# The opening of a fused hybrid-mixer step: modulation weights read in 512-column blocks, x and z weights behind them, z weights in pairs

## The chip, the cores and the metric

The kernel runs on one core of a Trainium2 chip. The metric is the device time of one execution in microseconds (us). Three runs of the kernel before took 2195.02, 2198.10 and 2202.01 us, the median 2198.1. Five engines work beside each other, each taking its own instructions in the order written: TensorE (PE), VectorE (DVE), ScalarE (ACT), GpSimd (POOL) and SyncE (SP), which issues most DMAs.

## What is computed

One layer for 2048 sample tokens and 128 prompt tokens, model width 1024. The part that matters here:

```python
def ada_mod(cvec, w, b):
    m = jnp.einsum('...d,de->...e', jax.nn.silu(cvec), w) + b
    return jnp.split(m, 3, axis=-1)                    # shift, scale, gate
...
xn = rmsnorm(h, ln_g[l]) * (1.0 + scale) + shift
...
proj = jnp.einsum('btd,de->bte', xn, w_in)             # one projection for everything
qkv, beta, dec, z_a, u_b, v_b, z_b, x_c, z_c, gates = jnp.split(proj, points, axis=-1)
qkv = short_conv(qkv, conv_w)                          # three taps along the tokens, then SiLU
...
o = rmsnorm(o, o_norm_g) * jax.nn.silu(z_a)            # z_a: 512 columns of w_in
```

Behind it stand a gated delta scan with decays made from `dec`, a spatial gating branch, a Fourier branch, the branch merge and the output projection. Shift and scale come from 1024 x 2048 numbers of `w_ada` and two condition vectors; every product of tokens and weights needs them first.

## The kernel before, in words

Tokens are processed in five tiles (`TBS`): four of 512 and one of 128. A float32 matrix enters TensorE as two float16 parts, so that one product is three matmuls: hi by hi, hi by lo, lo by hi. The token side is `xh` and `xl`, the weight side `w.hi` and `w.lo`.

**Stage one, the modulation** (the loop over `blk`). `w_ada` is read in eight blocks of 256 columns, each in two DMAs of 512 KB into one of eight `ast` buffers. TensorE multiplies the tiles by the condition (`scT`); for the blocks in `AD` the second tile is summed on VectorE instead (`ada_sum`) and brought in by two matmuls with `sel`. The first token tile is read in the middle, after block 4. `ms` (scale) and `sh` (shift) follow.

**Stage two, tokens and z** (the loop over `TBS`). For each token tile ScalarE squares (L451), POOL takes the power (L171), VectorE scales (L455), TensorE transposes in eight steps k (L459), VectorE applies scale and shift (`xm`, L461, three buffers), ScalarE rounds to `xh` (L462) and POOL subtracts to `xl` (L463). Then four z blocks of 128 columns are multiplied (L161) and their SiLU is stored to DRAM (`sz`).

**Stage three, q, k and v** (the loop over `ct`, twelve blocks of 128 columns). A block is 24 matmuls (8 steps by three) for each of five token tiles, the evacuation to `raw` (L635), three VectorE instructions for the convolution (L638, L639, L640, to `cy`), four Sigmoid pieces (L643, on ScalarE) and a POOL product. Beside it runs `decays()`, in pieces that `pace` doles out: matmuls with `bdp`, then 17 tiles of two 128x1024 VectorE instructions (L610, L611), one Exp (L598) and a DMA. Its Exp and the Sigmoid need different ScalarE tables, so tables are reloaded between them.

**Weights.** Every weight block is loaded to `wst` (two buffers, freed when converted), squared on ScalarE (L209), given a scale by a few tiny VectorE instructions and one TensorE matmul with `ones`, then converted: `hi` on ScalarE (L222), `lo` on VectorE (L223). `converting` is a generator; `weight_step`, `getw`, `fetch` and `ahead` decide when its steps are issued in the program.

**Order.** What one engine does first is not what the text says first: a scheduler puts the instructions of each engine in order when the program is built, from priorities (program order, with `tc.high_priority` ahead) and its own estimate of time. On the chip each engine then keeps to that order. `tc.issue_after(x)` holds a DMA behind another instruction.

Of the kernel before, what the change touches and what calls it, by code (L numbers as in the profile page):

```python
# [11 lines left out]
F16 = mybir.dt.float16  # L12
# [8 lines left out]
P = 128  # L21
D = 1024
KT = 8
# [88 lines left out]
def hybrid_flow_kernel(ctx: ExitStack, tc: tile.TileContext, x_prompt, x_sample, state_delta, c, c_ctx, ln_g, w_ada,  # L112
# [47 lines left out]
    def mm(out, l, r, start=True, stop=True):  # L160
        PE.matmul(out, l, r, start=start, stop=stop)  # L161

    def mm3(out, l, r):
# [2 lines left out]
        mm(out, l[0], r[1], False, False)  # L166
        mm(out, l[1], r[0], False, True)

    def rsqrt(out, ss, mul, w):
        V.tensor_scalar(out, ss, mul, EPS, ALU.mult, ALU.add)  # L170
        G.tensor_tensor(out, out, mhalf.to_broadcast([P, w]), ALU.pow)  # L171
# [18 lines left out]
    def load_w(src, nkt, cols=P, hi=None, lo=None, tag="w", bufs=5):  # L190
        return convert(read_w(src, nkt, cols, tag), nkt, cols, hi, lo, tag, bufs)

    def read_w(src, nkt, cols=P, tag="w"):
        st = sb(wp, [P, nkt, cols], "wst" if cols == P else tag + "st", bufs=2 if cols == P else 1)
        SY.dma_start(st, src.rearrange("(k p) c -> p k c", p=P))
        return st

    def converting(w, st, nkt, cols=P, hi=None, lo=None, tag="w", bufs=5):

        wpool = bwp[0] if tag == "b" else wp  # L200
        if tag == "z":
            hi, lo = [sb(p0p, [P, nkt, cols], n_, F16, bufs=4) for n_ in ("zhi", "zlo")]
# [19 lines left out]
        A.activation(w.hi, st, AF.Copy, scale=s)  # L222
        V.scalar_tensor_tensor(w.lo, st, s, w.hi, ALU.mult, ALU.subtract)  # L223
# [27 lines left out]
    def xrows(t0, n):  # L251
        return xs_[t0:t0 + n, :] if t0 < NS else xp_[t0 - NS:t0 - NS + n, :]

    wlist = []
    for c0 in [C_ZA + g * P for g in range(4)]:
        wlist.append((w_in_[:, c0:c0 + P], KT, "z", 4))
# [134 lines left out]
    def load_x(t0, tn):  # L391
        xt = sb(p0p, [P, tn // P, D], "xt")
        SY.dma_start(xt, xrows(t0, tn).rearrange("(j p) d -> p j d", p=P))
        xts[t0] = xt

    for blk in range(8):
        if blk == XB:
            load_x(*TBS[0])
            columns()
        ps = bank(ps_d, [2, 256])  # L400
        for k0 in range(0, KT, 4):
            st = sb(p0p, [P, 4, 256], "ast", bufs=8)
            last_ada = SY.dma_start(st, w_ada_[k0 * P:(k0 + 4) * P, blk * 256:(blk + 1) * 256].rearrange("(k p) c -> p k c", p=P))
            if k0 and blk in AD:
                acc = sb(p0p, [P, 2, 256], "aacc")
                ada_sum(acc, st, range(k0, k0 + 4))
                for g in range(2):
                    mm(ps, sel[:, g, :], acc[:, g, :], False, g == 1)
                continue
            for k in range(4):  # L410
                mm(ps, scT[:, k0 + k, :], st[:, k, :], k0 + k == 0, k0 + k == KT - 1)
        adr = sb(p0p, [2, 256], "adr")
        V.tensor_copy(adr, ps)
        for k in range(2):
            PE.transpose(pa[:, blk * 2 + k, :], adr[:, k * P:(k + 1) * P], ident[:2, :2])
    ms = sb(cp, [P, KT, 2], "ms")
    sh = sb(cp, [P, KT, 2], "sh")
    with tc.high_priority():
# [12 lines left out]


    szD = dram("sz", [H, P, NTOK])
    with tc.issue_after(last_ada.ins):
        read_next()
        read_next()
        load_x(*TBS[1])
        zaw = getw(4)
        bdp = sb(wp, [P, KT, 32], "bdp", F16, bufs=1)
        bdw = load_w(w_in_[:, C_BD:C_BD + 16], KT, 16, hi=bdp[:, :, 0:16], lo=bdp[:, :, 16:32], tag="d")  # L440
    szlate = []
    for ti, (t0, tn) in enumerate(TBS):
        if t0 not in xts:
            load_x(t0, tn)
        g = 0 if t0 < NS else 1
        nt = tn // P
        xt = xts[t0]
        jk = sb(p0p, [P, D], "jk", F16, bufs=1)
        xss = sb(p0p, [P, nt], "xss")
        for j in range(nt):  # L450
            A.activation(jk, xt[:, j, :], AF.Square, accum_out=xss[:, j:j + 1])  # L451
        rs = sb(p0p, [P, nt], "rs")
        rsqrt(rs, xss, 1.0 / D, nt)
        for j in range(nt):
            V.tensor_scalar(xt[:, j, :], xt[:, j, :], rs[:, j:j + 1], None, ALU.mult)  # L455
        for k in range(KT):
            ps = bank(ps_d, [P, tn])
            for j in range(nt):
                PE.transpose(ps[:, j * P:(j + 1) * P], xt[:, j, k * P:(k + 1) * P], ident)  # L459
            t = sb(p0p, [P, tn], "xm", bufs=3)  # L460
            V.tensor_scalar(t, ps, ms[:, k, g:g + 1], sh[:, k, g:g + 1], ALU.mult, ALU.add)  # L461
            A.copy(xh[:, k, t0:t0 + tn], t)  # L462
            G.tensor_tensor(xl[:, k, t0:t0 + tn], t, xh[:, k, t0:t0 + tn], ALU.subtract)  # L463
        for g in range(4):
            ps = bank(ps_d if tn == P and g % 2 else ps_mm, [P, tn])
            gemm_T(ps, zaw[g], 0, xh[:, :, t0:t0 + tn], xl[:, :, t0:t0 + tn])
            sg = sb(ep, [P, tn], "sg", bufs=4)
            A.activation(sg, ps, AF.Sigmoid, scale=zaw[g].inv)
            V.scalar_tensor_tensor(sg, ps, zaw[g].inv, sg, ALU.mult, ALU.mult)
            if szlate:  # L470
                SY.dma_start(*szlate.pop())
            szlate.append((szD[g, :, t0:t0 + tn], sg))
    SY.dma_start(*szlate.pop())
    p0.close()
    ahead(2)
# [173 lines left out]
    SY.dma_start(wsn, w_spatial[0].rearrange("g p q -> p g q"))  # L649
    pace.drain()  # L650
    a1.close()

# [909 lines left out]
```

## Time and profile before

| | |
|---|---|
| runs | 2195.02, 2198.10, 2202.01 us; median 2198.1 us |
| profiled execution | 2200.34 us, of which 2198.2 us are the span of the instructions |
| TensorE | 97% busy |
| VectorE, ScalarE, POOL | 60%, 46%, 32% busy |
| DMA | 365.09 MB, mean 166 GB/s |

Times inside the program count from the start of the span. A row of a timeline gives start, duration, engine, source line, operation, tiles written <- tiles read, shape, count and, in brackets, how long the engine had been idle and what ended that. A row of "windows" gives a stretch, its length, the busy time and count of PE, PEld (weight loads), DVE, ACT and POOL, the granted TensorE clock, the busy share of the DMA engines and GB/s. A row of the waits gives who waited for whom: total, times, longest.

### The profile page before, as it was taken

The page shows a single profiled execution, that of the slowest core. Times are in us where ns is not written, and L with a number is a line of the kernel's source. Part 1 is how long each engine was busy: PE and PEld are TensorE (multiplying, and loading weights), DVE is VectorE, ACT ScalarE, POOL GpSimd, SP SyncE. Part 2 cuts the span into 40 slices and gives each one's busy share as a digit, 9 for nine tenths or more (in the row PEclk, how much of TensorE's full clock was granted, in tenths as well). Part 3 has the DMA queues.
Part 4 walks back from the last instruction along what each step waited for, and adds up shares of the span by engine and source line. Part 5 has one row for each costly group of instructions (what it writes and reads, how often), then busy time and mean ns, then how long its engine had stood idle before and what let it go on. Part 6 is the DMA issues. An engine that isn't in the chain of part 4 may idle for free. (4 is left out here: it accounts for less than half of the span.)

```text
span 2198.2 us, 42667 instructions
## 1 busy us (share of the span) xinstructions
PE 2125.9 (97%) x16234; PEld 1213.1 (55%) x16234; DVE 1311.2 (60%) x3140; ACT 1014.4 (46%) x2345; POOL 707.5 (32%) x862
## 2 busy tenths in 40 slices
PE   7999999999999999899899999999999999999998
PEld 3565444455555587777555555555654444444443
DVE  5746745469979698466665555765674544223454
ACT  3644644345466474355544445655553422222332
POOL 1421433223333322432322223344532221222543
PEclk9999999999999999999999999999999999999999
DMA  8324733167777662444655556776664544324542
GB/s 280 141 87 149 260 117 110 61 203 231 241 229 239 198 192 83 126 130 137 203 172 162 164 164 185 240 212 209 200 198 151 168 125 133 118 78 123 174 148 103
DMA packets 304568, 365.09 MB, mean 166 GB/s; under 512 B 39426, under 2 KB 215787, under 8 KB 302315
## 3 DMA queue, kind: packets, MB, share of 16 engines
q1 hardware_dynamic: 289226, 302.19, 45.6%
q0 software_dynamic: 12688, 51.27, 6.4%
q10 hardware_dynamic: 2448, 8.91, 1.0%
q8 instruction: 127, 2.08, 0.4%
q14 instruction: 79, 0.64, 0.1%
HBM read 234.67 MB, written 127.62 MB: 165 GB/s over the span
## 5 line engine op out<-in xcount | busy, mean ns | idle before, releaser
L161 PE MATMUL b<-xh,whi 128*128 128x512 f16 (+1 forms) x1920 | 652.8, 349 | 0.4 <-DVE mrow L1391 0.4
L161 PE MATMUL b<-xl,whi 128*128 128x512 f16 (+1 forms) x1920 | 652.9, 348 | 0.0
L161 PE MATMUL b<-xh,wlo 128*128 128x512 f16 (+1 forms) x1920 | 651.9, 348 | 0.5 <-DVE wlo L223 0.5
L161 PEld LDWEIGHTS <-whi 128*128 128x128 f16 x3904 | 358.8, 98 | 330.0 <-issue 9.4
L161 PEld LDWEIGHTS <-wlo 128*128 128x128 f16 x1952 | 191.7, 98 | 180.8 <-issue 5.0
L161 PE MATMUL b<-big,bhi 128*128 128x512 f16 (+1 forms) x960 | 250.6, 347 | 2.4 <-ACT big L1355 1.9
L1395 POOL TENSOR_TENSOR mrow<-mrow,sg 128x512 f32<-128x512 f32 (+1 forms) x80 | 91.8, 1148 | 293.9 <-DVE sg L1394 225.7
L161 PE MATMUL b<-big,blo 128*128 128x512 f16 (+1 forms) x480 | 162.9, 347 | 0.0
L1385 ACT ACTIVATE sg<-b,winv 128x512 f32<-128x512 f32 (+1 forms) x120 | 74.1, 618 | 174.5 <-PE b L161 173.7
L644 POOL TENSOR_TENSOR cy<-cy,raw 128x545 f32<-128x545 f32 (+1 forms) x48 | 74.9, 1586 | 184.2 <-ACT raw L643 184.2
L161 PEld LDWEIGHTS <-xh 128*128 128x128 f16 x1496 | 117.0, 98 | 28.1
L1394 DVE SCALAR_TENSOR_TENSOR sg<-b,binv,sg 128x512 f32<-128x512 f32 (+1 forms) x80 | 53.4, 667 | 126.1 <-PE b L161 119.3
L161 PEld LDWEIGHTS <-bhi 128*128 128x128 f16 x960 | 86.5, 98 | 73.6 <-issue 2.1
L175 DVE CAST wscb<-wss 128x1 bf16<-128x1 f32 x93 | 14.3, 154 | 148.5 <-ACT wlo L209 67.3
L864 POOL COPY T<-ES 32x256 f16<-32x256 f16 x68 | 30.5, 449 | 202.3 <-DMA ES<-ei 167.1
L161 PE MATMUL b<-whi,xh 128*128 128x128 f16 x544 | 92.9, 219 | 0.0
L161 PE MATMUL b<-wlo,xh 128*128 128x128 f16 x544 | 92.9, 219 | 0.0
L161 PE MATMUL b<-whi,xl 128*128 128x128 f16 x544 | 92.9, 219 | 0.0
L161 PE MATMUL b<-wohi,mh 128*128 128x512 f16 x240 | 90.9, 379 | 1.4 <-ACT mh L1462 1.4
L161 PE MATMUL b<-wohi,ml 128*128 128x512 f16 x240 | 90.8, 379 | 0.3 <-DVE mscb L175 0.3
L161 PE MATMUL b<-wolo,mh 128*128 128x512 f16 x240 | 90.9, 379 | 0.0
L209 ACT ACTIVATE wlo<-wst 128x1024 f16<-128x1024 f32 x52 | 55.0, 1057 | 77.5 <-DMA wst<-in_w_in_dram 74.1
(456 smaller groups left out, 4285.4 us busy)
## 6 DMA issues: line engine op xcount, KB each, us to landing
wst<-in_w_in_dram SPq DMA_DIRECT2D x60, 512.0 KB, 4.9
qkv<-cy POOLq DMA_DIRECT2D x12, 1089.0 KB, 5.4
st<-br SPq DMA_DIRECT2D x48, 256.0 KB, 4.6
mrow<-mrg SPq DMA_DIRECT2D x18, 512.0 KB, 3.6
mrow<-mrg SPq DMA_DIRECT2D x16, 576.0 KB
mrg<-mrow POOLq DMA_DIRECT2D x16, 576.0 KB, 3.6
dc<-dec SPq DMA_DIRECT2D x17, 512.0 KB, 4.7
kq<-qkv SPq DMA_DIRECT2D x34, 256.0 KB, 4.6
```

The lines of the kernel that those rows point to most:

```text
L161: PE.matmul(out, l, r, start=start, stop=stop)
L175: V.tensor_copy(sb16, ss)
L209: A.activation(w.lo, st, AF.Square, accum_out=ss)
L644: G.tensor_tensor(y[:, c0:c1], y[:, c0:c1], raw[:, 1 + c0:1 + c1], ALU.mult)
L864: G.tensor_copy(T16[rows(a0, b), :, :, b], ES[0:32, :, 2 * a0 + b, :, wT])
L1385: A.activation(sg, ps, AF.Sigmoid, scale=gw.inv)
L1394: V.scalar_tensor_tensor(sg, ps, binv[:, 1:2], sg, ALU.mult, ALU.mult)
L1395: G.tensor_tensor(mr, mr, sg, ALU.add)
```

## The change

- The modulation is read in four blocks of 512 columns, each in four DMAs of two row groups (still 512 KB, rows of 2 KB instead of 1 KB). Of blocks 0 and 2 three of four tiles are summed on VectorE (before: one of two tiles of every other 256-column block).
- The first token tile is read after the modulation, in four pieces. Behind it come the z weights, in two pairs of 256 columns read into `ast` buffers (`read_z`), the second token tile, the weights for the decays, and only then (`issue_after(first[0])`) the first q block's weights.
- A pair of z blocks has one common scale and is converted in two halves (`convert_z`). For the first tile both blocks of a pair go through the contraction together.
- The squares of the next token tile, of the z weights and of the first q weights are pinned behind the ten ScalarE instructions before them in the program (`pinned`); the next tile is normalised after the first z block of the present one.

The core of the diff:

```diff
-XB = 4
-AD = (0, 2, 4, 6)
+AD = (0, 2)
...
+    def pinned(made, n=10):
+        ins = made.ins
+        before = (i for i in reversed(nc.cur_bb.bb.instructions) if i is not ins and i.engine == ins.engine)
+        for _, i in zip(range(n), before):
+            tc.add_manual_dep(ins, i.name, mybir.DependencyInfo(mybir.DependencyClass.NoSync, mybir.DependencyReason.DATA),
+                              reason="pinned")
+        return made
...
-        SY.dma_start(st, src.rearrange("(k p) c -> p k c", p=P))
+        with tc.issue_after(first[0]) if len(wread) < 8 and first else ExitStack():
+            SY.dma_start(st, src.rearrange("(k p) c -> p k c", p=P))
...
-        A.activation(w.lo, st, AF.Square, accum_out=ss)
+        sq = A.activation(w.lo, st, AF.Square, accum_out=ss)
+        if wnext[0] < 6:
+            pinned(sq)
...
-    for blk in range(8):
-        if blk == XB:
-            load_x(*TBS[0])
+    for blk in range(4):
+        if blk == 2:
             columns()
-        ps = bank(ps_d, [2, 256])
-        for k0 in range(0, KT, 4):
-            st = sb(p0p, [P, 4, 256], "ast", bufs=8)
+        ps = bank(ps_d, [2, 512])
+        acc = sb(p0p, [P, 2, 512], "aacc", bufs=1) if blk in AD else None
+        for k0 in range(0, KT, 2):
+            st = sb(p0p, [P, 2, 512], "ast", bufs=8)
...
-            if k0 and blk in AD:
+            if k0 and acc is not None:
+                ada_sum(acc, st, range(k0, k0 + 2), k0 == 2)
...
+    def convert_z(sts):
+        hi, lo = [sb(p0p, [P, KT, 256], n_, F16) for n_ in ("zhi", "zlo")]
+        ss = sb(p0p, [P, 3], "zss")
+        halves = [slice(4 * h, 4 * h + 4) for h in range(2)]
+        for h, kk in enumerate(halves):
+            pinned(A.activation(lo[:, kk, :], sts[h], AF.Square, accum_out=ss[:, h:h + 1]))
+        V.tensor_add(ss[:, 2:3], ss[:, 0:1], ss[:, 1:2])
+        s, inv = scales(ss[:, 2:3], wp, "wsc")
...
     with tc.issue_after(last_ada.ins):
-        read_next()
-        read_next()
+        xt = sb(p0p, [P, 4, D], "xt")
+        for j in range(4):
+            SY.dma_start(xt[:, j, :], xrows(j * P, P))
+        xts[0] = xt
+        zst = [read_z(0), read_z(1)]
         load_x(*TBS[1])
-        zaw = getw(4)
...
+    fetch(4)
...
+        convert_z(zst[1])
+        for g0 in (0, 2):
+            pss = [bank(ps_mm, [P, tn]) for _ in range(2)]
+            for k in range(KT):
+                x_ = [t_[:, k, t0:t0 + tn] for t_ in (xh, xl)]
+                for i in range(2):
+                    mm(pss[i], zaw[g0 + i].hi[:, k, :], x_[0], k == 0, False)
+                    mm(pss[i], zaw[g0 + i].lo[:, k, :], x_[0], False, False)
+                for i in range(2):
+                    mm(pss[i], zaw[g0 + i].hi[:, k, :], x_[1], False, k == KT - 1)
+            if g0 == 0:
+                xt = next_x(ti)
```

The rebuilt order differs from the start of the program up to the middle of stage three; from the fourth q block's first tile to the end the instructions of TensorE stand as before. Lines move by up to 83: L161 becomes L160, L222 and L223 become L231 and L232, L610 and L611 become L692 and L693, L635 becomes L717, L638 to L640 become L720 to L722, L643 becomes L725.

**First place: the weights of the third q block (`ct` 2) on ScalarE and VectorE.** Before, ScalarE converts them (`whi_1984`, and the fourth block's `whi_2168`) in stage two, during the third and fourth token tile:

```order
L468 ACTIVATE sg_979<-b_954,winv_367 128x512
L462 CAST xh_93<-xm_1032 128x512
L462 CAST xh_93<-xm_1041 128x512
L462 CAST xh_93<-xm_1050 128x512
L222 ACTIVATE whi_1984<-wst_1848,wsc_2080 128x1024
L222 ACTIVATE whi_2168<-wst_2034,wsc_2263 128x1024
L468 ACTIVATE sg_1008<-b_983,winv_386 128x512
```

Now ScalarE converts the same two blocks (`whi_1911`, `whi_2095`) in stage three, behind the Sigmoid pieces of the second q block (`cy_2144`) and an Exp of the decays (`XB`):

```order
L725 ACT_TABLE_LOAD
L725 ACTIVATE raw_1931<-cy_2144 128x545 x3
L725 ACTIVATE raw_1931<-cy_2144 128x543
L680 ACT_TABLE_LOAD
L680 ACTIVATE XB_1874<-XB_1874 128x1024
L231 ACTIVATE whi_1911<-wst_1775,wsc_2007 128x1024
L680 ACTIVATE XB_1874<-XB_1874 128x1024
L231 ACTIVATE whi_2095<-wst_1961,wsc_2190 128x1024
```

The two conversions have moved by more than sixty ScalarE rows, from before the first q block to after the second one's Sigmoid.

VectorE before, from the second block's last convolution instruction (`cy_2217`) on, has no weight block until the third block's own convolution:

```order
L640 SCALAR_TENSOR_TENSOR cy_2217<-raw_2004,pc_108,cy_2217 128x2178
L611 TENSOR_TENSOR XB_1947<-XB_1947,cst_87 128x1024 x2
L610 TENSOR_TENSOR dc_2038<-dc_2038,tok_1768 128x1024
L610 TENSOR_TENSOR dc_2045<-dc_2045,tok_1768 128x1024
L611 TENSOR_TENSOR dc_2038<-dc_2038,cst_87 128x1024
L611 TENSOR_TENSOR dc_2045<-dc_2045,cst_87 128x1024
L610 TENSOR_TENSOR E_2087<-E_2087,tok_1768 128x1024
```

VectorE now, from the second row behind that convolution instruction (the row between is one more L693 on `XB_1874`) to the third block's `lo` part (`wlo_1912`):

```order
L194 TENSOR_SCALAR wsc_2007<-wsc_2007 128x1
L195 TENSOR_SCALAR wsc_2007<-wsc_2007 128x1
L693 TENSOR_TENSOR XB_1874<-XB_1874,cst_87 128x1024
L194 TENSOR_SCALAR wsc_2190<-wsc_2190 128x1
L195 TENSOR_SCALAR wsc_2190<-wsc_2190 128x1
L692 TENSOR_TENSOR dc_1965<-dc_1965,tok_1695 128x1024
L692 TENSOR_TENSOR dc_1972<-dc_1972,tok_1695 128x1024
L229 TENSOR_TENSOR winv_2012<-wsc_2007,xsc_246 128x1
L229 TENSOR_TENSOR winv_2195<-wsc_2190,xsc_246 128x1
L693 TENSOR_TENSOR dc_1965<-dc_1965,cst_87 128x1024
L692 TENSOR_TENSOR E_2014<-E_2014,tok_1695 128x1024
L232 SCALAR_TENSOR_TENSOR wlo_1912<-wst_1775,wsc_2007,whi_1911 128x1024
```

The `lo` part now stands behind six instructions of the decays that follow the second block's convolution, the last of them on a fresh `E` tile. On TensorE the third block still follows the second at once; of its matmuls the first two (hi by `xh`, hi by `xl`) of each of its five tiles and of the fourth block's first tile now stand ahead of the first one that reads `wlo_1912`.

**Second place: the weights of the first q block (`ct` 0) on ScalarE.** Before, they were converted in stage two, and at the start of stage three ScalarE has the Exp on `al` (a small parameter that is loaded there) and evacuations:

```order
L468 ACTIVATE sg_1384<-b_1359,winv_386 128x128
L540 ACT_TABLE_LOAD
L540 ACTIVATE al_1772<-al_1772 128x8
L635 ACTIVATE raw_1452<-b_1456,winv_1448 128x512
L523 COPY sq_1486<-b_1487 128x144
L523 COPY sq_1486<-b_1634 128x128
```

Now the conversion stands behind that Exp:

```order
L216 ACTIVATE wlo_1361,wss_1362<-wst_1358 128x1024
L622 ACT_TABLE_LOAD
L622 ACTIVATE al_1699<-al_1699 128x8
L605 COPY sq_1413<-b_1414 128x144
L231 ACTIVATE whi_1360<-wst_1358,wsc_1368 128x1024
L717 ACTIVATE raw_1377<-b_1381,winv_1373 128x512
```

The square and the `hi` part of the first q block have moved from stage two to behind the last z block. On TensorE most of the decays' `bdp` matmuls now stand ahead of the first block's matmuls instead of behind its first tile.

More of the change, by code (lines that the diff above doesn't have):

```diff
@@ L252, in xrows @@
         return xs_[t0:t0 + n, :] if t0 < NS else xp_[t0 - NS:t0 - NS + n, :]
-    wlist = []
-    for c0 in [C_ZA + g * P for g in range(4)]:
-        wlist.append((w_in_[:, c0:c0 + P], KT, "z", 4))
+    wlist, first = [], []
+    wlist.extend([None] * 4)
     for c0 in ([C_QKV + i * P for i in range(12)] + [C_V + g * P for g in range(4)]
@@ L433, in hybrid_flow_kernel, with read_z @@
     szD = dram("sz", [H, P, NTOK])
-    with tc.issue_after(last_ada.ins):
-        read_next()
-        read_next()
+    def read_z(pair):
+        sts = []
+        for h in range(2):
+            st = sb(p0p, [P, 4, 256], "ast", bufs=8)
+            first[:] = [SY.dma_start(st, w_in_[h * 512:(h + 1) * 512, C_ZA + pair * 256:C_ZA + (pair + 1) * 256].rearrange("(k p) c -> p k c", p=P)).ins]
+            sts.append(st)
+        return sts
+    def convert_z(sts):
[6 more added lines that the diff above has]
+        s, inv = scales(ss[:, 2:3], wp, "wsc")
+        zinv = sb(wp, [P, 1], "winv", bufs=10)
+        V.tensor_mul(zinv, inv, isx)
+        for h, kk in enumerate(halves):
+            A.activation(hi[:, kk, :], sts[h], AF.Copy, scale=s)
+            V.scalar_tensor_tensor(lo[:, kk, :], sts[h], s, hi[:, kk, :], ALU.mult, ALU.subtract)
+        for i in range(2):
+            w = _W()
+            w.hi, w.lo, w.inv = hi[:, :, i * P:(i + 1) * P], lo[:, :, i * P:(i + 1) * P], zinv
+            zaw.append(w)
@@ L437, in hybrid_flow_kernel @@
+    zaw = []
+    with tc.issue_after(last_ada.ins):
+        xt = sb(p0p, [P, 4, D], "xt")
[3 more added lines that the diff above has]
+        zst = [read_z(0), read_z(1)]
         load_x(*TBS[1])
-        zaw = getw(4)
         bdp = sb(wp, [P, KT, 32], "bdp", F16, bufs=1)
-        bdw = load_w(w_in_[:, C_BD:C_BD + 16], KT, 16, hi=bdp[:, :, 0:16], lo=bdp[:, :, 16:32], tag="d")
-    szlate = []
[L442 to L446, printed above, removed]
+        bdst = read_w(w_in_[:, C_BD:C_BD + 16], KT, 16, "d")
@@ L447, in hybrid_flow_kernel, with normed @@
+    wdone.extend([None] * 4)
+    wread.extend([None] * 4)
+    wnext[0] = 4
+    fetch(4)
+    szlate = []
+    def normed(t0, tn, step):
         xt = xts[t0]
         jk = sb(p0p, [P, D], "jk", F16, bufs=1)
[L449 to L472, printed above, removed]
+        for j0 in range(0, tn // P, step):
+            js = range(j0, min(j0 + step, tn // P))
+            xss = sb(p0p, [P, len(js)], "xss")
+            for j in js:
+                sq = A.activation(jk, xt[:, j, :], AF.Square, accum_out=xss[:, j - j0:j - j0 + 1])
+                if t0:
+                    pinned(sq)
+            rs = sb(p0p, [P, len(js)], "rs")
+            rsqrt(rs, xss, 1.0 / D, len(js))
+            for j in js:
+                V.tensor_scalar(xt[:, j, :], xt[:, j, :], rs[:, j - j0:j - j0 + 1], None, ALU.mult)
@@ new lines, in normed, with z_out, next_x @@
+        return xt
+    def z_out(g, t0, tn, ps):
+        sg = sb(ep, [P, tn], "sg", bufs=4)
+        A.activation(sg, ps, AF.Sigmoid, scale=zaw[g].inv)
+        V.scalar_tensor_tensor(sg, ps, zaw[g].inv, sg, ALU.mult, ALU.mult)
+        if szlate:
+            SY.dma_start(*szlate.pop())
+        szlate.append((szD[g, :, t0:t0 + tn], sg))
+    def next_x(ti):
+        if ti + 1 == len(TBS):
+            return None
+        if TBS[ti + 1][0] not in xts:
+            load_x(*TBS[ti + 1])
+        return normed(*TBS[ti + 1], 4)
@@ new lines, in hybrid_flow_kernel @@
+    xt = normed(*TBS[0], 2)
+    with tc.high_priority():
+        convert_z(zst[0])
+    for ti, (t0, tn) in enumerate(TBS):
+        m = 0 if t0 < NS else 1
+        nt = tn // P
+        with tc.high_priority() if ti == 0 else ExitStack():
+            for k in range(KT):
+                ps = bank(ps_d, [P, tn])
+                for j in range(nt):
+                    PE.transpose(ps[:, j * P:(j + 1) * P], xt[:, j, k * P:(k + 1) * P], ident)
+                t = sb(p0p, [P, tn], "xm", bufs=3)
+                V.tensor_scalar(t, ps, ms[:, k, m:m + 1], sh[:, k, m:m + 1], ALU.mult, ALU.add)
+                A.copy(xh[:, k, t0:t0 + tn], t)
+                G.tensor_tensor(xl[:, k, t0:t0 + tn], t, xh[:, k, t0:t0 + tn], ALU.subtract)
+        if ti:
+            for g in range(4):
+                ps = bank(ps_d if tn == P and g % 2 else ps_mm, [P, tn])
+                gemm_T(ps, zaw[g], 0, xh[:, :, t0:t0 + tn], xl[:, :, t0:t0 + tn])
+                z_out(g, t0, tn, ps)
+                if g == 0:
+                    xt = next_x(ti)
+            if ti == 1:
+                bdw = convert(bdst, KT, 16, hi=bdp[:, :, 0:16], lo=bdp[:, :, 16:32], tag="d")
+            continue
+        convert_z(zst[1])
+        for g0 in (0, 2):
+            pss = [bank(ps_mm, [P, tn]) for _ in range(2)]
+            for k in range(KT):
+                x_ = [t_[:, k, t0:t0 + tn] for t_ in (xh, xl)]
+                for i in range(2):
+                    mm(pss[i], zaw[g0 + i].hi[:, k, :], x_[0], k == 0, False)
+                    mm(pss[i], zaw[g0 + i].lo[:, k, :], x_[0], False, False)
+                for i in range(2):
+                    mm(pss[i], zaw[g0 + i].hi[:, k, :], x_[1], False, k == KT - 1)
+            if g0 == 0:
+                xt = next_x(ti)
+            for i in range(2):
+                z_out(g0 + i, t0, tn, pss[i])
@@ L648, in hybrid_flow_kernel @@
     wsn = sb(ep, [P, WB], "st", bufs=3).rearrange("p (g q) -> p g q", g=4)
-    SY.dma_start(wsn, w_spatial[0].rearrange("g p q -> p g q"))
+    with tc.issue_after(first[0]):
+        SY.dma_start(wsn, w_spatial[0].rearrange("g p q -> p g q"))
     pace.drain()
```

19 lines of the change are left out of this document (8 added, 11 removed).

## The prediction, made blind

> **What bounds the kernel now.** I read the page's engine rows first, then TensorE's waits, then windows over the part that the change touches.
>
> ```profile
> span 2198.2 us, 42667 instructions
> PE 2125.9 (97%) x16234; PEld 1213.1 (55%) x16234; DVE 1311.2 (60%) x3140; ACT 1014.4 (46%) x2345; POOL 707.5 (32%) x862
> 0.00:64.00 64.00, 47.30 (x218) 21.07 (x219) 36.30 (x94) 23.19 (x43) 14.84 (x19) 0.97 0.84 275
> 64.00:260.00 196.00, 196.00 (x1347) 105.08 (x1346) 122.49 (x179) 104.88 (x161) 65.25 (x60) 1.00 0.46 151
> PE b L161 <- DVE wlo L223: 0.5, 1, 0.5
> 200.00:220.00 20.00, 20.00 (x112) 9.82 (x111) 19.53 (x14) 13.45 (x17) 8.06 (x4) 1.00 0.77 249
> ```
>
> TensorE is the bound, so a microsecond in which it waits is a microsecond of the program. The first 64 us are the exception: DMA share 0.84, and most of the busy matmuls are the small modulation ones. From 64 to 260 us TensorE has no gap, and in the waits of 64 to 300 us there is one of 0.5 us (fifth row). But beside it VectorE is nearly full at 200 to 220 us (19.53 of 20). The kernel gets away with that because no weight that TensorE needs next stands behind VectorE's backlog. That is what the change alters, so my sum has a small term at the start and a large one there.
>
> **Part one: the start.** It has to bring 0.4 MB of constants, 8.4 MB of modulation and 2.1 MB of the first token tile, before and now. The rates:
>
> ```profile
> 0.00:8.00 8.00, 1.16 (x4) 0.51 (x5) 0.17 (x1) 1.47 (x2) 0.61 (x9) 1.00 0.66 213
> 8.00:16.00 8.00, 8.00 (x27) 2.47 (x26) 3.60 (x10) 0.00 (x0) 0.00 (x0) 1.00 1.10 351
> 16.00:22.00 6.00, 6.00 (x31) 2.45 (x30) 3.11 (x8) 0.00 (x0) 0.00 (x0) 1.00 1.04 396
> 58.00:62.00 4.00, 3.46 (x19) 1.64 (x16) 4.00 (x3) 1.44 (x6) 4.00 (x3) 1.00 1.02 419
> 23.26 1.06 ACT L451 ACTIVATE jk<-xt 128x1024 f16<-128x1024 f32 x1 [18.54 <-DMA xt<-in_x_sample_dram]
> 28.24 1.18 POOL L171 TENSOR_TENSOR rs<-rs,mhalf 128x4 f32<-128x4 f32 x1 [27.03 <-DVE rs L170]
> 29.45 2.74 DVE L455 TENSOR_SCALAR xt<-xt,rs 128x1024 f32<-128x1024 f32 x4
> 43.65 0.17 DVE L420 TENSOR_TENSOR sh<-b,pc 128x16 f32<-128x16 f32 x1 [0.84 <-PE b L415]
> 46.22 0.80 DVE L461 TENSOR_SCALAR xm<-b,ms,sh 128x512 f32<-128x512 f32 x1
> 48.65 6.62 POOL L463 TENSOR_TENSOR xl<-xm,xh 128x512 f16<-128x512 f32 x4 [19.23 <-ACT xh L462]
> 63.14 0.38 PE L161 MATMUL b<-xl,zhi 128*128 128x512 f16 x1
> ```
>
> Rows of 1 KB move at 351 GB/s (8 to 16 us, modulation alone), rows of 4 KB at 419 (58 to 62 us, a token tile): 46.7 and 156.4 ns a row on 16 engines. On the line between them 2 KB take 83.3 ns, 393 GB/s. By 8 us 1.7 MB had moved; the rest of the modulation then ends at 8 + 7.1/0.393 = 26.1 us, the token tile at 31.1, the first z pair (1 KB rows) at 34.1. What has moved is used some 1.8 us later: 6.7 MB stand ahead of the token tile's first use now, moved by 21.5 us and used at 23.26. So the tile's last quarter is usable at 32.9. Then, in VectorE's new order: a square 1.2, the power (1.18) with a 0.64 us copy of modulation rows ahead of it 2.0, two scalings 1.4 (2.74 for four), and the 2.6 from `sh` to `xm` (43.65 to 46.22): first `xm` at 40.1 instead of 46.2.
>
> Of these 6 us little reaches TensorE. ScalarE now squares the z weights only behind the bound on `ms` and `sh` (2 x 1.2 us), so the first `xl` starts at about 42.0. `xm` has three buffers, each freed by its `xl`; VectorE's order has the seventh `xm` ahead of the first z `lo` part, so that part waits for four `xl` (1.2 to 1.65 us each by the POOL row), one `xm` and 1.27 us: 49 to 51. From there 46 matmuls of the first pair, 48 of the second and 32 transposes are left, at 0.216 and 0.109 us each (the step from 206.04 to 206.26, and some 1.1 us for the ten transposes at 99.17, both below). Before, TensorE had done the first pair and nine of the transposes at 63.1, so in the same terms the work was left at 63.1 - 9.9 - 1.0 = 52.2 us. TensorE is also cold then:
>
> ```profile
> 46.00:48.00 2.00, 0.92 (x5) 0.80 (x6) 2.00 (x9) 2.00 (x4) 0.00 (x0) 0.75 0.00 0
> 48.00:50.00 2.00, 2.00 (x10) 1.74 (x10) 2.00 (x3) 2.00 (x4) 1.35 (x1) 0.50 0.00 0
> 50.00:52.00 2.00, 1.68 (x7) 0.50 (x5) 2.00 (x3) 2.00 (x5) 2.00 (x2) 0.90 0.43 100
> ```
>
> After a thin stretch its granted clock falls to 0.50 and needs some 3.4 us of work to recover, which costs 1.7 us where matmuls are waiting, as they will be now. Term: 50 + 1.7 - 52.2 = **-0.5** (from -6, the lead of `xm` kept whole, to +2).
>
> A rule speaks against the longer rows. The Trainium skill, "DMA: Bandwidth & Descriptors", section "Where 436 GB/s comes from", has about 358 GB/s per core bind for reads from HBM. By it the modulation would end about 2 us later than I have it; the 419 GB/s above, a read from HBM, disagrees.
>
> **Part two: the tile borders.** Before, the second and fourth token tiles were transposed ahead of the last z block of the tile before; now every tile is transposed after it. The one large border that already had that order:
>
> ```profile
> 99.17 1.25 PE L459 MATMUL b<-cst,xt 128*128 128x128 f32 x10
> 101.11 0.59 PE L161 MATMUL b<-xh,zhi 128*128 128x512 f16 x2
> 102.34 0.38 PE L161 MATMUL b<-xl,zhi 128*128 128x512 f16 x1
> ```
>
> Here 3.2 us pass for 2.7 us of work. With the first step's transposes, an `xm` (0.8) and an `xh` (0.6) all ahead of the first matmul I put 0.8 at three borders and 0.3 at the small tile, less the 0.5 there now: **+2.2** (0 to 4).
>
> **Part three: the first q block's weights.** Their `hi` part now stands behind the Exp on `al`:
>
> ```profile
> 159.03 1.28 ACT L540 ACT_TABLE_LOAD   x1 [4.16 <-DMA al<-in_a_log_dram]
> 154.24 0.22 PE L161 MATMUL b<-xh,zlo 128*128 128x128 f16 x1
> L161 PE MATMUL b<-bdp,xl x68: 169/169/169, 162.8 to 166.2; 128*128 128x16 f16 x68
> L161 PE MATMUL b<-bdp,xh x67: 176/176/176, 162.9 to 166.2; 128*128 128x32 f16 x67
> ```
>
> The load of `al` is issued behind the last `sz` store, so it comes no earlier against the end of stage two: `al` at 159.0, table 1.28, Exp 0.2, copy 0.3, `hi` 1.14: 161.9. TensorE has 192 `bdp` matmuls of 0.025 us to do from 154.3, that is to 159.1, and then waits: **+2.8** (0 to 5).
>
> **Part four: the third q block's weights.** This is the prediction's weight. Rows of before, around the end of the second q block:
>
> ```profile
> 205.99 0.22 PE L161 MATMUL b<-xh,wlo 128*128 128x128 f16 x1
> 206.04 0.38 PE L161 MATMUL b<-xh,whi 128*128 128x512 f16 x1
> 206.26 0.38 PE L161 MATMUL b<-xl,whi 128*128 128x512 f16 x1
> 191.53 2.36 DVE L610 TENSOR_TENSOR dc<-dc,tok 128x1024 f32<-128x1024 f32 x2 [6.82 <-DMA dc<-gamR]
> 212.97 2.24 DVE L638 TENSOR_SCALAR cy<-raw,pc 128x2178 f32<-128x2178 f32 x1
> 215.19 2.10 DVE L611 TENSOR_TENSOR dc<-dc,cst 128x1024 f32<-128x1024 f32 x1
> 226.01 2.48 DVE L640 SCALAR_TENSOR_TENSOR cy<-raw,pc,cy 128x2178 f32<-128x2178 f32 x1
> 237.04 1.45 DVE L610 TENSOR_TENSOR E<-E,tok 128x1024 f32<-128x1024 f32 x1 [1.75 <-DMA E<-gamR]
> 247.95 1.28 DVE L223 SCALAR_TENSOR_TENSOR wlo<-wst,wsc,whi 128x1024 f16<-128x1024 f32 x1
> 227.56 1.28 ACT L643 ACT_TABLE_LOAD   x1 [0.39 <-ACT E L598]
> 228.86 1.21 ACT L643 ACTIVATE raw<-cy 128x545 f32<-128x545 f32 x2
> 233.04 2.00 ACT L598 ACTIVATE XB<-XB 128x1024 f32<-128x1024 f32 x2
> 245.79 1.14 ACT L222 ACTIVATE whi<-wst,wsc 128x1024 f16<-128x1024 f32 x1
> ```
>
> TensorE ends the second block at 206.0 and goes straight on, since the third block's weights were converted long ago. VectorE works without a pause from 191.5 and ends that block's convolution only at 228.4. Now the third block's `hi` part stands behind that block's Sigmoid. VectorE's rows from the first `dc` to that convolution are the same plus some tiny ones (0.7 us): 229.1. Four Sigmoid pieces 2.4, table 1.3, Exp 1.0, `hi` 1.14: 235.0. The `lo` part stands behind six decay instructions, the last of them on the `E` tile that came by DMA at 237.04; with the 0.7 us 237.7, plus 1.45 and 1.28: 240.5. Between 206.0 and then TensorE has the twelve early matmuls, ten of 0.216 and two of 0.055, 2.3 us. Term: 240.5 - 206.0 - 2.3 = **+32.2**. A shift of everything ahead moves both ends alike. What is queued behind the waiting matmul is all the rest of the program, and no other work is offered to TensorE.
>
> It cannot be nothing: the Sigmoid needs the second block's convolution, which needs that block's last matmul. Without any backlog: evacuation 0.4, the three convolution instructions 1.35 + 2 x 2.48, five decay instructions between them at 1.2, seven more and `lo` 9.0, less 2.3: 19.5. From above: the six behind at the 2.1 us that such an instruction takes beside POOL (215.19) and 3 us more for `E`: 40.6.
>
> After more than 30 us without work the clock is at 0.50 once more: **+1.7** (0 to 2).
>
> **Sum.** -0.5 + 2.2 + 2.8 + 32.2 + 1.7 = +38.4. On the profiled execution's 2200.3 us (span 2198.2) this is 2238.7; that execution lies 2.2 above the median of 2198.1, so I predict 2236 for the median.
>
> **Rivals.**
> - *VectorE is abreast* at the second block's end, and the wait is its shortest, 19.5: 2198.1 + 6.2 + 19.5 = 2224. For it: ScalarE and DMA have slack at 180 to 200. Against: VectorE's start there waits for the `gamR` loads (6.82 us), which the change does not bring forward. Chance 0.17.
> - *A second wait.* The fifth q block's weights are loaded only when the third's are converted, about 241; they need a load of 5 us, a place on ScalarE behind two Exp and one on VectorE behind the third block's convolution, by my count about 268, when TensorE wants them at 282. If that margin of 14 is used up, 10 to 20 more: 2251. Chance 0.08.
> - *Not slower.* The new weights' `hi` part is ready before the second block ends, at 206.0 instead of 235.0. That needs the order on ScalarE not to bind, 29 us earlier than its place allows. Then the start decides, with the lead of `xm` kept: 2198.1 - 6 + 2.2 = 2194. Against: VectorE's rows of before stand in the trace exactly as ordered. Chance 0.04.
> - *Reads capped*, by that page's figure: the 2 KB rows run at the 351 GB/s of the 1 KB rows, and the modulation ends 2.2 us later: 2238. The 419 GB/s speaks against it. Chance 0.03.
>
> **How the numbers follow.** Forecast 0.68. The range takes the low ends of the start and the wait without adding them all (2214, which holds the first rival) and the high end of the wait with some of the borders (2250); the second wait, the not-slower case and the far ends stay out. A change of 0.3%, 6.6 us, is about what a measurement of this kernel can tell from none. Faster 0.03, same 0.03, slower 0.94.
>
> **What would show it.** Right: first `xm` near 40 us; TensorE without a gap from about 52 to 155; a wait of about 3 us on ScalarE's `hi` near 159; then one wait of some 30 us, put down to the `hi` and `lo` parts of the third q block, near 210 to 243. Wrong: no such wait, or TensorE fed by other rows there; or gaps in stage two larger than the lead.

## The result, and the profile after

The changed kernel takes 2239.15 us (median of 6 runs, 2237.43 to 2245.5) beside 2200.55 us for the kernel before (6 runs, 2195.02 to 2208.55): 1.018 of it, 95% interval 1.0162 to 1.0197, **1.8% slower**. The prediction was 2236.

The page's engine row, and three windows of the changed kernel in the columns shown above (from 64 to 260 us the kernel before had no gap on TensorE):

```profile
PE 2129.8 (95%) x16168; PEld 1209.7 (54%) x16168; DVE 1308.6 (59%) x3119; ACT 1015.0 (45%) x2343; POOL 692.7 (31%) x863
64.00:154.00 90.00, 86.71 (x496) 46.08 (x495) 43.12 (x71) 37.85 (x71) 33.50 (x35) 1.00 0.21 77
200.00:220.00 20.00, 15.13 (x88) 7.54 (x87) 18.64 (x14) 9.37 (x13) 0.00 (x0) 1.00 0.62 198
220.00:240.00 20.00, 0.23 (x2) 0.10 (x1) 19.41 (x20) 12.82 (x16) 9.42 (x9) 0.50 0.90 288
```

Between 220 and 240 us TensorE works for 0.23 us, while VectorE is busy for 19.41 of the 20: the hole is not an idle chip, it is TensorE standing behind VectorE's row of work. TensorE's waits over the first 300 us say what it stood for (who waited for whom, total, times, longest):

```profile
PE b L160 <- ACT whi L231: 25.0, 2, 21.3
PE b L160 <- DVE wscb L183: 8.1, 2, 7.9
PE b L526 <- DVE xm L528: 4.6, 5, 2.0
PE b L160 <- DVE wlo L232: 2.2, 1, 2.2
```

The 21.3, the 7.9 and the 2.2 are three parts of one hole of 31.4 us, with a few matmuls between them: TensorE stands for the scale, the `hi` part and the `lo` part of the third q block's weights. The names alone would blame ScalarE. The timeline from 214 to 252 us shows what each part stood behind:

```profile
214.91 0.22 PE L160 MATMUL b<-xh,wlo 128*128 128x128 f16 x1
223.07 0.23 PE L160 MATMUL b<-wscb,ones 128*128 128x1 bf16 x2 [7.94 <-DVE wscb L183]
236.03 2.47 DVE L722 SCALAR_TENSOR_TENSOR cy<-raw,pc,cy 128x2178 f32<-128x2178 f32 x1
238.81 2.30 ACT L725 ACTIVATE raw<-cy 128x545 f32<-128x545 f32 x4
241.13 1.28 ACT L680 ACT_TABLE_LOAD   x1
242.42 1.06 ACT L680 ACTIVATE XB<-XB 128x1024 f32<-128x1024 f32 x1
243.39 1.13 ACT L231 ACTIVATE whi<-wst,wsc 128x1024 f16<-128x1024 f32 x1
244.57 0.61 PE L160 MATMUL b<-xh,whi 128*128 128x512 f16 x1 [21.28 <-ACT whi L231]
241.82 4.13 DVE L692 TENSOR_TENSOR dc<-dc,tok 128x1024 f32<-128x1024 f32 x2
248.11 1.21 DVE L692 TENSOR_TENSOR E<-E,tok 128x1024 f32<-128x1024 f32 x1
249.24 1.27 DVE L232 SCALAR_TENSOR_TENSOR wlo<-wst,wsc,whi 128x1024 f16<-128x1024 f32 x1
250.57 0.51 PE L160 MATMUL b<-xh,wlo 128*128 128x512 f16 x1 [2.23 <-DVE wlo L232]
250.88 0.63 PE L160 MATMUL b<-xh,whi 128*128 128x512 f16 x1
251.31 0.63 PE L160 MATMUL b<-xl,whi 128*128 128x512 f16 x1
```

TensorE ends the second block at 215.1. VectorE ends that block's convolution at 238.5 (the row at 236.03); then come four pieces of its Sigmoid on ScalarE, a table load, one Exp, and only then `hi`, at 244.5. `lo` stands behind the decay instruction on `E` and comes at 250.5. This is the chain that the prediction wrote down, each link 9 to 10 us later because TensorE itself is 9 us later there.

### The profile page after: what moved, and what is told of

Same layout as the page of the kernel before. It is cut to its first block, busy times and chain, and to the rows that moved or that the text cites. A ratio compares the mean times of both kernels' runs of the same rounds, so it can differ in the third digit from the quotient of the medians.

```text
span 2235.4 us, 42523 instructions
## 1 busy us (share of the span) xinstructions
PE 2129.8 (95%) x16168; PEld 1209.7 (54%) x16168; DVE 1308.6 (59%) x3119; ACT 1015.0 (45%) x2343; POOL 692.7 (31%) x863
## 5 line engine op out<-in xcount | busy, mean ns | idle before, releaser
L160 PE MATMUL b<-xh,whi 128*128 128x512 f16 (+1 forms) x1920 | 654.9, 350 | 26.2 <-ACT whi L231 25.0
L160 PE MATMUL b<-xl,whi 128*128 128x512 f16 (+1 forms) x1920 | 655.1, 350 | 0.0
L160 PE MATMUL b<-xh,wlo 128*128 128x512 f16 (+1 forms) x1920 | 652.2, 349 | 2.2 <-DVE wlo L232 2.2
L160 PEld LDWEIGHTS <-whi 128*128 128x128 f16 x3904 | 359.6, 98 | 358.1 <-ACT whi L231 25.3
L160 PEld LDWEIGHTS <-wlo 128*128 128x128 f16 x1952 | 191.9, 98 | 182.2 <-issue 5.3
L160 PE MATMUL b<-big,bhi 128*128 128x512 f16 (+1 forms) x960 | 251.1, 348 | 4.1 <-ACT big L1438 2.7
L160 PE MATMUL b<-big,blo 128*128 128x512 f16 (+1 forms) x480 | 163.2, 347 | 0.0
L160 PEld LDWEIGHTS <-xh 128*128 128x128 f16 x1496 | 117.6, 98 | 28.3 <-issue 0.3
L726 POOL TENSOR_TENSOR cy<-cy,raw 128x545 f32<-128x545 f32 (+1 forms) x48 | 62.1, 1320 | 210.4 <-ACT raw L725 210.4
L160 PEld LDWEIGHTS <-bhi 128*128 128x128 f16 x960 | 86.5, 98 | 74.8 <-issue 3.6
L160 PE MATMUL b<-whi,xl 128*128 128x128 f16 x544 | 92.9, 219 | 0.0
L160 PE MATMUL b<-whi,xh 128*128 128x128 f16 x544 | 92.9, 219 | 0.0
L160 PE MATMUL b<-wlo,xh 128*128 128x128 f16 x544 | 92.9, 219 | 0.0
L160 PE MATMUL b<-wohi,mh 128*128 128x512 f16 x240 | 90.9, 379 | 1.3 <-ACT mh L1545 1.3
L160 PE MATMUL b<-wohi,ml 128*128 128x512 f16 x240 | 90.8, 379 | 0.3 <-DVE mscb L183 0.3
L160 PE MATMUL b<-wolo,mh 128*128 128x512 f16 x240 | 90.9, 379 | 0.0
```

Of the source, the lines that this page charges most:

```text
L726: G.tensor_tensor(y[:, c0:c1], y[:, c0:c1], raw[:, 1 + c0:1 + c1], ALU.mult)
```

## The experiments

Theory A: the loss comes from the time at which the first q blocks' weights are converted, because the pin keeps their squares behind the last ScalarE work of the z stage; with the two `wst` buffers in use until then, the third and fourth follow later still. Theory B: VectorE's backlog would hold TensorE in any case. Theory C: the new start and the later transposes cost it. The kernel before took 2197.0 us beside runs 1 to 4 and beside runs 5 to 8, and 2196.8 beside the two repeats in run 4.

**1. The changed kernel without the pin on the q weights' squares.**

```diff
         sq = A.activation(w.lo, st, AF.Square, accum_out=ss)
-        if wnext[0] < 6:
-            pinned(sq)
```

> The changed kernel without the pin on the square of the q blocks' weights, and nothing else. Theory A (the weights of the first four q blocks are converted too late, and that is the loss): their hi and lo parts are written during the z stage again; the 30 us wait near 215 to 250 and the 3.8 us wait near 160 both go, with the two cold restarts behind them (about 2 us each): 2239 - 33 - 6 = 2200, within 5. The squares now stand early on ScalarE, so the start may move by up to 3. Theory B (VectorE's decay backlog holds the third block and the weights are only named last): within 6 of 2239. Theory C (the new start and the later transposes cost most of it): 2225 or more.

Measured: 2201.06 us, 1.0021 of before (1.0011 to 1.0031). Both waits on `whi` are gone; TensorE has no gap from 154 to 300 us. Theory A holds to 1.1 us.

**2. The pins stay, but the weights are worked on in the z stage.**

```diff
                 if g == 0:
                     xt = next_x(ti)
+                if ti in (1, 2):
+                    fetch(4 + 2 * ti)
+                    for _ in range(2):
+                        weight_step()
```

> The changed kernel with its pins, but the q blocks' weights are worked on in the z stage: two weight steps behind each z block of the second and third token tile. Theory A: 2200, within 5, like the run without the pin, with the start exactly as in the changed kernel (first xm near 41.3). Theory B: within 6 of 2239. Theory C: 2225 or more. The extra small matmul of each weight may cost up to 2 in the z stage.

Measured: 2198.85 us, 1.0011 (1.0001 to 1.002). The four `hi` parts (the first is shown; the last starts at 139.72) now stand between the z blocks on ScalarE, and the stretch that was empty is full (timeline and windows of this run):

```profile
102.40 1.14 ACT L231 ACTIVATE whi<-wst,wsc 128x1024 f16<-128x1024 f32 x1
215.00:225.00 10.00, 10.00 (x49) 4.52 (x47) 6.60 (x4) 7.52 (x11) 5.30 (x4) 1.00 0.60 220
225.00:235.00 10.00, 10.00 (x55) 4.81 (x54) 10.00 (x9) 5.50 (x6) 2.26 (x5) 1.00 0.95 313
```

From 225 us on VectorE is as full as in the kernel before (10.00 of 10; in the 10 us ahead of that 6.60, where the kernel before has 10.00), and TensorE doesn't care: theory B falls. What is left of the change, start and borders together, is worth +1.8 us in the medians: theory C falls too. That small rest is not a stage two as fast as before, though: at the first transposes behind the q blocks (`kq`) this trace stands at 459.7 us, the kernel before at 452.6. Part of these 7 us is a cold restart at the border of the fourth token tile, where TensorE waits 0.95, 0.80 and 0.60 us within 6 us:

```profile
128.00:134.00 6.00, 5.40 (x21) 3.55 (x20) 5.26 (x11) 4.68 (x8) 3.54 (x4) 0.50 0.13 48
```

**3. The kernel before with the pin alone.** The function `pinned` is added as in the changed kernel, and:

```diff
-        A.activation(w.lo, st, AF.Square, accum_out=ss)
+        sq = A.activation(w.lo, st, AF.Square, accum_out=ss)
+        if tag == "w" and 4 < wnext[0] < 6:
+            pinned(sq)
```

> The kernel before with only the pin added to the squares of the first q blocks' weights; its start, its modulation blocks and its z order stay. Theory A: the whole loss appears without the rest of the change: a wait of 3 to 4 on the first q block's hi part near 158, a wait of some 30 on the third's, and a cold restart behind each: 2200.5 + 6 + 33 = 2239, within 6. Theory B: it depends on VectorE alone, whose work is the same: within 6 of 2200. Theory C: within 6 of 2200.

Measured: 2230.83 us, 1.0159 (1.0144 to 1.0174). The waits from 200 to 300 us:

```profile
PE b L161 <- ACT whi L233: 21.4, 1, 21.4
PE b L161 <- DVE wscb L184: 5.9, 1, 5.9
PE b L161 <- DVE wlo L234: 3.1, 1, 3.1
```

These 30.4 us are the long wait with nothing else of the change in the kernel. The short wait did not appear, which the expectation had wrong: here `hi` stands ahead of the Exp on `al`. 33.8 us were lost, 5 less than the expectation, which had 6 for the short wait.

**4. `dt_bias` and `a_log` loaded early** in the changed kernel, in buffers that live through the program, with the Exp behind `hi`:

```diff
...
-        SY.dma_start(al, a_log.rearrange("o d h -> o (d h)").to_broadcast([P, 8]).rearrange("p (d h) -> p d h", d=2))
-        A.activation(al, al, AF.Exp)
+        pinned(A.activation(al, al, AF.Exp))
...
     szlate = []
+    dtb, al = [sb(cp, [P, 2, H], n_) for n_ in ("dtb", "al")]
+    for t_, src in ((dtb, dt_bias), (al, a_log)):
+        SY.dma_start(t_, src.rearrange("o d h -> o (d h)").to_broadcast([P, 8]).rearrange("p (d h) -> p d h", d=2))
```

> The changed kernel with dt_bias and a_log loaded in the z stage and the Exp on a_log pinned behind the first q block's hi part; the third block's weights stay late. Prediction's reading (a wait of 3.8, no cold restart behind it): 3.8 less, 2235. Reading with a cold restart behind the short wait as well (the granted clock was 0.50 from 166 to 170): 5.5 to 6 less, 2233. Rival: the long wait ends at a time that VectorE sets alone, so the gain is swallowed there: within 1.5 of 2239.

Measured: 2233.51 us, 1.0167 (1.015 to 1.0183), which overlaps the changed kernel's interval. So both were measured once more on one chip:

> The changed kernel once more, as the yardstick for the next run on the same chip: 1.016 to 1.020 of the kernel before.

> The kernel with dt_bias and a_log loaded early once more, since three rounds left its interval overlapping that of the changed kernel. Its trace ends the second q block 4.6 earlier than the changed kernel's although its first xm came 1.8 later. Short wait with a cold restart behind it: 5.5 to 6 below the changed kernel. Wait of 3.8 alone: 3.8 below. Swallowed: within 1.5 of it.

The changed kernel took 2239.45 us, 1.0186 (1.0166 to 1.0206); with `al` early 2234.09, 1.0159 (1.0138 to 1.018). The intervals still overlap. The medians put the short wait at 5.4 us here, without deciding between 3.8 and 5.5; the trace shows why it can exceed the 3.8 us for which TensorE stands. In the changed kernel (timeline, then windows):

```profile
163.42 1.28 ACT L622 ACT_TABLE_LOAD   x1 [4.37 <-DMA al<-in_a_log_dram]
164.98 1.15 ACT L231 ACTIVATE whi<-wst,wsc 128x1024 f16<-128x1024 f32 x1
166.19 0.61 PE L160 MATMUL b<-xh,whi 128*128 128x512 f16 x1 [3.76 <-ACT whi L231]
166.00:170.00 4.00, 3.81 (x44) 2.02 (x45) 1.28 (x1) 0.13 (x1) 0.00 (x0) 0.50 0.31 82
170.00:174.00 4.00, 4.00 (x15) 1.57 (x14) 0.00 (x0) 0.00 (x0) 0.00 (x0) 0.72 0.18 53
```

and in the run with `al` early, where that wait is missing:

```profile
164.00:174.00 10.00, 10.00 (x95) 5.19 (x92) 2.43 (x9) 3.32 (x7) 0.00 (x0) 1.00 0.20 54
```

A wait of 3.76 us is followed by 4 us at half clock and 4 at 0.72. In the repeat of the changed kernel the wait is 2.96 us, and the clock falls to 0.50 behind it as well. The gain was not swallowed by the long wait, which is 31.4 us in the first run with `al` early too.

**5. The z squares without their pin**, on the kernel of run 2, which all of 5 to 7 start from:

```diff
-            pinned(A.activation(lo[:, kk, :], sts[h], AF.Square, accum_out=ss[:, h:h + 1]))
+            A.activation(lo[:, kk, :], sts[h], AF.Square, accum_out=ss[:, h:h + 1])
```

> The run with the weights in the z stage (2198.9), with the pin on the squares of the z weights taken off as well: they now stand on ScalarE ahead of the bound on ms and sh. Theory S (the lead of xm did not reach TensorE because those squares, and with them the scale and the hi and lo parts of the first z pair, stand behind the bound and the first xm): the first z hi part comes near 42 instead of 46.6, the first lo part near 46 instead of 49.6, and 3 (2 to 4) are gained: 2196. Rival P (GpSimd's eight xl, 1.2 each from 42.9, hold the first tile in any case): within 1 of 2198.9.

Measured: 2197.56 us, 1.0003 (0.9991 to 1.0015). The parts moved as theory S said:

```profile
42.05 2.19 ACT L462 ACTIVATE zhi<-ast,wsc 128x1024 f16<-128x1024 f32 x2 [1.39 <-DVE wsc L194]
44.56 3.38 DVE L463 SCALAR_TENSOR_TENSOR zlo<-ast,wsc,zhi 128x1024 f16<-128x1024 f32 x2
```

The time moved by 1.3, at the edge of the rival's 1: not decided by the time. The trace decides it for theory S: by 63.1 us 71 z matmuls of the first tile have started, against 56 in run 2, which is 3.2 us of work, and the eight `xl` did not hold them.

**6. The third and fourth token tiles squared and transposed earlier.**

```diff
-                if t0:
+                if t0 == 512:
                     pinned(sq)
...
+    def turn(ti, xt):
+        t0, tn = TBS[ti]
...
                 if g == 0:
                     xt = next_x(ti)
+                if g == 2 and ti + 1 < len(TBS):
+                    turn(ti + 1, xt)
```

(`turn` is the loop of transposes, `xm`, `xh` and `xl`, which the program had at the head of each tile.)

> The run with the weights in the z stage (2198.9), with the third and fourth token tiles squared and transposed ahead of the last z block of the tile before, as the kernel before had it. Reading of the prediction (0.8 to 1 lost at each border, the xm waits of 2.8 in all): two borders saved, 1.5 to 2.5 less, 2197. Rival (the borders are hidden elsewhere): within 0.7 of 2198.9.

Measured: 2196.52 us, 0.9993 (0.9983 to 1.0002): 2.3 less, as the border reading has it, though its interval and that of run 2 just touch. The edit also moves the small fifth tile forward, so three borders change. In the trace the gain has two parts: shorter borders, and the clock of run 2's fourth tile, which stays at 1.00 from 64 to 154 us here.

**7. Both.**

> Both edits on the run with the weights in the z stage. If S and the border reading hold and add up: 2198.9 - 3 - 2 = 2194, that is 0.15% below the kernel before. If neither holds: 2198.9.

Measured: **2190.16 us, 0.996 (0.9946 to 0.9975)**: faster than both kernels, and more than the two gains added. TensorE works for 88.34 of the 90 us in which the changed kernel had 86.71 and run 2 had 85.17:

```profile
64.00:154.00 90.00, 88.34 (x534) 49.12 (x533) 52.54 (x100) 42.91 (x79) 34.23 (x41) 1.00 0.29 97
```

In the traces, where the first transposes behind the q blocks start, runs 5, 6 and 7 are at 455.6, 454.0 and 448.0 us, against 459.7 of run 2: 4.1 and 5.7 gained alone, 11.7 together, 2 more than the sum. Only run 7 is ahead of the kernel before there (452.6). What the total shows of these gains comes and goes in a later stage (next section).

**8. The decay work spread out**, in the changed kernel with its late weights:

```diff
-    pace.start(decays(), 1.2)
+    pace.start(decays(), 4.0)
```

> The changed kernel, weights still late, with the decay work spread over the q blocks at one piece for 4.0 us of TensorE's work instead of 1.2. ScalarE's order then has the third block's hi part ahead of the second block's Sigmoid, and VectorE's has its lo part behind ten decay instructions instead of some twenty and two convolutions. Theory (the wait is as long as the row of work that stands ahead of the third block's conversion on VectorE and ScalarE): the wait shrinks from 31 to about 10 (4 to 20): 2218, from 2208 to 2228. Rival (the weights come late by their own load and square): the wait stays near 30: 2236 or more.

Measured: 2210.69 us, 1.006 (1.0042 to 1.0078). The waits from 156 to 300 us and the place of the conversion:

```profile
PE b L160 <- ACT whi L231: 8.8, 2, 5.5
219.10 1.14 ACT L231 ACTIVATE whi<-wst,wsc 128x1024 f16<-128x1024 f32 x1
220.27 1.29 DVE L232 SCALAR_TENSOR_TENSOR wlo<-wst,wsc,whi 128x1024 f16<-128x1024 f32 x1 [1.10 <-ACT whi L231]
```

The long wait is 5.5 us, and `hi` and `lo` are finished at 220.2 and 221.6. The weights' loads are issued when they were (from 168.5 us, 167.5 in the changed kernel); what went is the row of work ahead of the conversion. The third block's square starts at 195.2 instead of 217.8 us, its `hi` part stands ahead of the second block's Sigmoid, and its `lo` part ahead of that block's convolution (from 221.6 on). So the wait's length is that row, and this one constant takes back some 28 us of the loss.

## Why the prediction was right, step by step

The accounts can be closed at the first transposes behind the q blocks (first of the rows of one form; then the first and last `Q` of the recurrence, before and after):

```profile
L698 PE MATMUL b<-cst,kq x136: 271/273/332, 452.6 to 826.0; 128*128 128x128 f32 x136
L781 PE MATMUL b<-cst,kq x136: 270/273/329, 495.9 to 868.5; 128*128 128x128 f32 x136
L862 ACT ACTIVATE Q<-b x34: 372/373/374, 920.6 to 1624.7; 32x256 f16<-32x256 f32 x34
L945 ACT ACTIVATE Q<-b x34: 372/373/373, 962.9 to 1662.2; 32x256 f16<-32x256 f32 x34
```

The changed kernel is 43.3 us late there. By the prediction's terms:

| term | predicted | measured |
|---|---|---|
| the start | -0.5 | -3.2: at 63.1 us 57 z matmuls of the first tile are done; before, 38 and nine transposes |
| tile borders | +2.2 | 5.6: from there to the end of stage two the steps between matmuls exceed their usual 0.216 and 0.109 us by 6.1 in all, by 0.5 before |
| first q block's `hi` behind `al` | +2.8 | 3.8, and 2.5 more at the lower clock (twelve 128x512 matmuls start 0.38 to 0.43 us apart) |
| third q block's weights | +32.2 | 31.4 |
| cold restart after them | +1.7 | 3.0 (sixteen such matmuls) |
| sum | +38.4 | 43.1 |

The first three come to 8.7, and the second block's last matmul does start 8.9 later, at 214.91 instead of 205.99. The sum is 0.2 short of the 43.3.

**Right in mechanism and size:** the long wait. The kernel before with the pin alone shows it without the shift of the start: the convolution ends at 227.8 (229.1 predicted), `hi` at 233.8 (235.0), `lo` at 240.8 (240.5):

```profile
225.32 2.47 DVE L651 SCALAR_TENSOR_TENSOR cy<-raw,pc,cy 128x2178 f32<-128x2178 f32 x1
232.68 1.13 ACT L233 ACTIVATE whi<-wst,wsc 128x1024 f16<-128x1024 f32 x1
239.54 1.28 DVE L234 SCALAR_TENSOR_TENSOR wlo<-wst,wsc,whi 128x1024 f16<-128x1024 f32 x1
```

**Right in its path, wrong in its reference:** the start. The first `xm` came at 41.34 (40.1 predicted), the first z `lo` at 48.15 to 49.6 (49 to 51):

```profile
41.34 2.25 DVE L528 TENSOR_SCALAR xm<-b,ms,sh 128x512 f32<-128x512 f32 x3
42.88 5.62 POOL L530 TENSOR_TENSOR xl<-xm,xh 128x512 f16<-128x512 f32 x5 [5.88 <-ACT xh L529]
46.60 2.19 ACT L462 ACTIVATE zhi<-ast,wsc 128x1024 f16<-128x1024 f32 x2
47.42 0.81 DVE L528 TENSOR_SCALAR xm<-b,ms,sh 128x512 f32<-128x512 f32 x1
48.15 1.43 DVE L463 SCALAR_TENSOR_TENSOR zlo<-ast,wsc,zhi 128x1024 f16<-128x1024 f32 x1
```

The path is the one that was written down: five `xl` take 5.62 us, 1.12 each; the fourth ends near 47.4, the seventh `xm` starts at 47.42, and `lo` follows it at 48.15, with its `hi` ready at 47.7. What was wrong is the kernel before as reference. The prediction has the first pair's 48 matmuls done there at 63.1 us; the rows (timeline of before up to 63.1) add up to 38:

```profile
L161 PE MATMUL b<-xh,zhi x14: 379/379/634, 48.8 to 61.1; 128*128 128x512 f16 x14
L161 PE MATMUL b<-xl,zhi x12: 376/378/379, 50.8 to 60.4; 128*128 128x512 f16 x12
L161 PE MATMUL b<-xh,zlo x12: 377/379/389, 51.3 to 60.6; 128*128 128x512 f16 x12
```

Ten matmuls of 0.216 are 2.2 us, so its sum for the start, done with 38, gives -2.6. The changed kernel really is ahead when stage two begins.

**Mis-sized: the borders.** 5.6 lies outside the 0 to 4 that were given, and it eats that lead. At the third tile's border 16 transposes, 1.7 us of work by their usual step, take the 3.76 us from 97.04 to 100.80. The weight loads that go with the transposes (PEld, waits from 64 to 154 us) name the cause: they wait for VectorE, which takes the results away (`xm`) and scales the tokens (`xt`), 5.4 us in all:

```profile
97.04 2.22 PE L526 MATMUL b<-cst,xt 128*128 128x128 f32 x12
PEld b L526 <- DVE xm L528: 4.0, 5, 1.2
PEld b L526 <- DVE xt L498: 1.4, 4, 0.4
```

The busy time hides part of it: from 64 to 154 us it leaves only 3.3 us idle, since a transpose's row (0.27 us) is longer than its step. The prediction took 0.5 from a border of the kernel before and added 0.3; the start and the borders were wrong by 2.7 and 3.4 in opposite directions, and that the two nearly cancel is luck.

**Mis-sized: the restarts.** The first q block's wait was 3.8 instead of 2.8, and the prediction gave a cold restart to the long wait only. The short one has one as well, of 2.5 (1.3 in the repeat of the changed kernel), and the long one lost 3.0.

**Not foreseen:** 43.3 us at 453 us have become 37.1 at the end of the profiled executions. From the first to the last `Q`, 704.1 us passed before and 699.3 after; in the other kernels between 698.8 and 703.0. The repeat of the changed kernel shows how little that says: the same program took 703.3 us there. So most of the 4.8 us lies within what one kernel scatters from one execution to the next, and a gain from arriving later isn't shown. This later stage is why the total came 3 us from the forecast although the terms ahead add up to 5 more; that closeness too is partly luck. The medians of the changed kernel are 38.6 and 42.7 us above before.

Of the rivals, VectorE was not abreast, no second wait came at the fifth q block, and the reads were not capped (below), though the modulation ended late: its last rows landed at 28.8 us (26.1 predicted), after a stretch of 269 GB/s from 16 to 20 us with the DMA engines 0.84 busy.

## What to carry to other kernels

An edit that delays work nobody waits for at that place can move it behind a backlog further on: follow what is moved to the queue in which it lands, and price the whole row ahead of it, not its own duration. Ask of every pin or added wait which buffers stay occupied behind it, since the loads that need them move too. A gain at the start is worth what the stages behind it let through: here 5 us of lead for `xm` became 3 at TensorE, and the tile borders took them back until the squares and the transposes moved as well. Count what is done at a reference time matmul by matmul, and judge a border by the steps between matmuls, not by the busy time.

## What the runs showed of the hardware

- A short wait can cost its cold restart too: 3.76 us of waiting, then 0.50 of the clock for 4 us and 0.72 for 4 more. The Trainium skill, "TensorE: Matmul & The Clock Gate", section "Part 1: The HAM clock gate (the "warmup" mystery)", has the array throttle after an idle window of about 3.4 us; the 3.76 us agree, but shorter waits lowered the clock here too: 2.96 us in the repeat of the changed kernel, the 2.23 us of the next point, and the three of less than 1 us each in run 2 (0.50 from 128 to 134 us). The border waits of the changed kernel, up to 1.0 us, left it at 1.00 (64 to 154 us), and so did one of 3.35 us in run 6 (up to 77.73). So the length of one wait does not decide it alone.
- The long wait restarts the clock more than once: the matmuls from 244.57 on (0.61 us each, where 0.38 is usual) are cold, and those from 250.88, behind the 2.23 us for `lo`, are cold again and start 0.43 us apart (250.88 and 251.31). By the steps between them 1.3 and 1.7 us are lost, 3.0 instead of the 1.7 predicted. In the repeat `lo` came after 1.34 us, the clock did not fall a second time, and 2.4 us were lost.
- Reads of 2 KB rows (the modulation, in the changed kernel) moved at 399 GB/s from 24 to 28 us:

```profile
24.00:28.00 4.00, 2.73 (x8) 0.59 (x8) 4.00 (x8) 0.00 (x0) 0.00 (x0) 1.00 1.05 399
```

The cap of about 358 GB/s that was weighed in the prediction did not bind with one core at work. From 8 to 16 us the same rows moved at 356 GB/s, hardly faster than the 1 KB rows of the kernel before (351).
